# Twelve weight operands of the first four up-projection pairs, made beside the branch projections and brought by way of DRAM

## The chip, the cores and the metric

One program runs on one core of a Trainium2 chip. The metric is the device time of the program in microseconds (us), the median of several runs. Within the core five engines work side by side, each through its own instructions in order: TensorE (PE, matmuls; its weight loads are PEld), VectorE (DVE), ScalarE (ACT), GpSimd (POOL) and SyncE (SP). DMAs are issued by SP, ACT and POOL and then run by themselves. Engines wait for one another through semaphores.

## What is computed

The reference is one layer of an encoder on 1024 positions of width 1024. Its first half mixes positions by three branches, whose outputs are projected (`w_branch`), gated and added; its second half is a gated feed-forward with a conv of width 3. The two places that the change touches are these:

```python
def _token_mixer(...):
    ...
    branches = jnp.stack([o_a, o_b, o_c], axis=2)
    up = jnp.einsum('bsnw,nwd->bsnd', branches, w_branch)
    gates = jax.nn.sigmoid(gate_raw.reshape(bn, s, N_BRANCH, D_MODEL) + b_gate)
    return jnp.sum(gates * up, axis=2) @ w_o

def _conv_ffn(h, w_up, conv_w, conv_b, w_down):
    hu = _dwconv(h @ w_up, conv_w, FFN_CONV // 2) + conv_b
    a, b = jnp.split(hu, 2, axis=-1)
    return (jax.nn.silu(a) * b) @ w_down
```

`w_up` has 1024 rows and 2 x 2816 columns, which are 2 x 22 blocks of 128 columns.

## The kernel before

**Splitting.** A product of two float32 matrices is made of three matmuls. Each operand is split into a high part (a cast, on ACT) and a low part (the operand less the high part, on DVE or POOL); the matmuls are high by high, low by high and high by low. In the names `h` and `l` at the end say which part it is.

**The up-projection** goes through 22 pairs `p`: block `p` of `w_up` (of the half that goes through silu) and block 22 + `p` (the half that it is multiplied with). One pair is a 2 by 2 block matrix: two column blocks by two halves of the contraction, four raw blocks that the code calls a, b (of block `p`) and c, d (of block 22 + `p`), each 128 x 512 in memory. It is multiplied with a 2 by 2 block matrix of the activations by seven products instead of eight (`m1` to `m7`). So each pair needs operands that are sums of raw blocks: `P1` = c + d, `P3` = a + c, `P2` = P3 + d, `P4` = b + P2, besides the raw blocks A11, A12 (both in `wu1`) and A22 = d. The activations come as sums too (`T1` to `T4`, `B11`, `B21`, `B22`). A product is 12 matmuls. `m1` wants A11, `m2` A12, `m7` P3, `m6` P2, `m5` P1, `m3` A22, `m4` P4.

For each pair `up_load` (L1493) loads the two raw tiles `wur` (512 KB each) by SP and splits `wu1`; `sum_1` to `sum_4` (L1507 to L1525) make the sums in place or in `p2`; `w_split` (L1527) splits an operand, the cast on ACT and the subtraction on the engine that its caller names. For pair 2 and later `w_first` (L1536) makes P3 and P2, with sums and subtractions on DVE, and `w_later` (L1544) makes P1, A22 and P4, with sums on POOL. Pairs 0 and 1 are spread by hand over the end of the norm and the first products (L1722 to L1792), with their sums and subtractions on DVE (`pV`) and their casts on ACT (`pA`); their A22 and P4 lie in tiles named `wl`, which take buffers of the activations' tiles `F` as these come free. Each result runs through the conv (`conv`, L1795: one step on ACT and two on DVE, L1797 and L1798), and `gated` (L1807) multiplies the two halves (L1813) and stores `g_d`.

**The branch projections** of branches A and B run some 450 us before that (`ups`, L1168: 16 jobs of 24 matmuls, `up_steps`). Job by job, SP loads `wbr` (256 KB) and a gate tile (`load_gate`, L1137: 512 KB of `gt_d`, and a sigmoid on ACT, L1140); `wbr` is split into `wbh` on ACT and `wbl` on DVE; after the matmuls DVE multiplies the gate tile with the result (L1167); and after the second job of two POOL adds the two gate tiles (L1184) and stores the sum as `acc_d` (L1185). Between these matmuls run the preparations of branch C (`c_tab`, `c_prep`): transposes of `xc` into `cT`, which ACT and DVE split into `chi` and `clo` (L1104, L1105); `qpe` matmuls, whose rope is four DVE steps (L1025 to L1028) and two POOL adds (L1029, L1030); the split of the result (`n`, L1121 and L1122), its transposes `qpT`, and copies (`qp` L1096, `kpa` L1078).

**What sets the order.** TensorE's order is that of the program: where `T.kept` is set each matmul depends on the one before. Instructions that go through `pV` or `pA` keep their order among themselves in the same way. All others are placed by the framework's scheduler, which estimates when each is ready and lays out each engine's stream by that; what runs on the chip is that stream, in order. A step that waits holds up what stands behind it on its engine, the DMAs that the engine issues among them. A tile with `bufs=1` (the default where none is named) has one buffer, so its next writer waits for the last reader of the one before, for a DMA that reads it until that has landed.

## Time and profile before

| | |
|---|---|
| time, median of 3 runs | 1993.56 us (1991.68 to 1996.82) |
| the profiled execution, its own time | 1993.97 us |
| its span, first to last instruction | 1992.2 us |
| TensorE busy (matmuls) | 1928.9 us, 97% |
| TensorE's mean granted clock | 0.993 |
| DVE busy | 1280.6 us, 64% |
| ACT busy | 853.4 us, 43% |
| POOL busy | 419.7 us, 21% |
| DMA, mean | 105 GB/s |

The profile is of one execution. A row of a time line gives the start in the span, the duration, engine, line, operation, output<-inputs, and in brackets the time that the engine stood idle before and what ended that. A matmul's duration overlaps with the next one's start, so the distance of two starts is what one costs. The line of many instructions is that of a helper (L103 for those through `pV` and `pA`, L128 for matmuls, L131 for transposes, L166 and L169 for the split), so they are told apart by the tiles' names. The granted clock is a share of TensorE's full speed, 1.00 for 2.4 GHz.

### The profile page before, as it was taken

The page shows a single profiled execution, that of the slowest core. Times are in us where ns is not written, and L with a number is a line of the kernel's source. Part 1 is how long each engine was busy: PE and PEld are TensorE (multiplying, and loading weights), DVE is VectorE, ACT ScalarE, POOL GpSimd, SP SyncE. Part 2 cuts the span into 40 slices and gives each one's busy share as a digit, 9 for nine tenths or more (in the row PEclk, how much of TensorE's full clock was granted, in tenths as well). Part 3 has the DMA queues.
Part 4 walks back from the last instruction along what each step waited for, and adds up shares of the span by engine and source line. Part 5 has one row for each costly group of instructions (what it writes and reads, how often), then busy time and mean ns, then how long its engine had stood idle before and what let it go on. Part 6 is the DMA issues. An engine that isn't in the chain of part 4 may idle for free. (4 is left out here: it accounts for less than half of the span.)

```text
span 1992.2 us, 27009 instructions
## 1 busy us (share of the span) xinstructions
PE 1928.9 (97%) x10440; PEld 1606.6 (81%) x10440; DVE 1280.6 (64%) x2076; ACT 853.4 (43%) x1449; POOL 419.7 (21%) x338
## 2 busy tenths in 40 slices
PE   7998999999999999989999999998999999999998
PEld 6976887888888878868888887886888888888887
DVE  7378868666766736674467855588777677742523
ACT  6554544264254322354455543454444444532331
POOL 3321122041131111122200022103323333111110
PEclk9999999999999999999999999999999999999999
DMA  8443122122122127243500134213222222455641
GB/s 293 140 154 116 38 75 75 43 80 80 43 80 75 54 82 260 74 149 128 184 1 22 33 126 142 93 43 109 73 93 80 79 85 75 159 200 146 209 152 54
DMA packets 79203, 209.16 MB, mean 105 GB/s; under 512 B 11681, under 2 KB 17121, under 8 KB 79074
## 3 DMA queue, kind: packets, MB, share of 16 engines
q1 hardware_dynamic: 62514, 165.68, 26.2%
q10 hardware_dynamic: 14256, 33.36, 4.3%
q0 software_dynamic: 2304, 8.39, 1.1%
q8 instruction: 82, 1.34, 0.3%
q14 instruction: 47, 0.39, 0.1%
HBM read 165.62 MB, written 41.78 MB: 104 GB/s over the span
## 5 line engine op out<-in xcount | busy, mean ns | idle before, releaser
L128 PE MATMUL pj<-hhi,wth 128*128 128x512 f32 x704 | 293.8, 417 | 4.4 <-ACT u L895 1.7
L128 PE MATMUL pj<-hhi,wtl 128*128 128x512 f32 x704 | 276.8, 393 | 0.0
L128 PE MATMUL pj<-hlo,wth 128*128 128x512 f32 x704 | 275.6, 391 | 0.0
L128 PEld LDWEIGHTS pj<-hhi,wtl 128*128 128x128 f32 x704 | 132.5, 188 | 29.0
L128 PEld LDWEIGHTS pj<-hhi,wth 128*128 128x128 f32 x704 | 133.1, 189 | 25.7 <-ACT u L895 2.2
L128 PEld LDWEIGHTS pj<-hlo,wth 128*128 128x128 f32 x704 | 133.4, 189 | 20.0
L169 POOL TENSOR_TENSOR wtl<-wtr,wth 128x512 fp32r<-128x512 f32 x44 | 64.0, 1455 | 405.7 <-ACT wth L166 316.5
L169 DVE TENSOR_TENSOR gl<-gr,gh 128x512 fp32r<-128x512 f32 x38 | 29.5, 778 | 106.7 <-ACT gh L166 106.7
L128 PE MATMUL y<-wdh,gh 128*128 128x512 f32 x240 | 93.4, 389 | 0.0
L128 PE MATMUL y<-wdl,gh 128*128 128x512 f32 x240 | 93.4, 389 | 0.0
L128 PE MATMUL y<-wdh,gl 128*128 128x512 f32 x240 | 93.4, 389 | 0.0
L166 ACT CAST wth<-wtr 128x512 fp32r<-128x512 f32 x88 | 53.3, 617 | 85.8 <-PE pj L128 59.9
L128 PE MATMUL y<-wo,mg 128*128 128x512 f32 x384 | 89.2, 391 | 0.0
L605 ACT CAST tU<-pu 128x512 f16<-128x512 f32 x80 | 44.1, 587 | 102.4 <-PE pu L128 98.9
L128 PEld LDWEIGHTS y<-wo,mg 128*128 128x128 f32 x384 | 71.6, 188 | 14.7
L1520 POOL TENSOR_TENSOR wur<-wur 128x512 f32<-128x512 f32 x20 | 34.5, 1725 | 231.3 <-DVE wur L1509 192.6
L166 ACT CAST gh<-gr 128x512 fp32r<-128x512 f32 x38 | 23.7, 622 | 116.6 <-PE y L128 97.3
L610 DVE CAST tT<-pq 128x512 f16<-128x512 f32 x96 | 62.8, 684 | 16.4 <-PE pq L128 16.2
L599 DVE TENSOR_TENSOR pm<-pp,msk 128x512 f16<-128x512 f32 x96 | 63.4, 685 | 15.2 <-PE pp L128 14.5
L1388 POOL TENSOR_TENSOR g<-g,ac 128x1024 f32<-128x1024 f32 x7 | 18.4, 2629 | 217.8 <-DVE g L1167 211.2
L169 POOL TENSOR_TENSOR wdl<-wdr,wdh 128x1024 fp32r<-128x1024 f32 x12 | 29.3, 2442 | 153.7 <-ACT wdh L166 151.7
L433 ACT ACTIVATE gate<-pj,b_gate 128x512 f32<-128x512 f32 x48 | 32.9, 685 | 56.2 <-PE pj L128 56.0
(572 smaller groups left out, 5388.1 us busy)
## 6 DMA issues: line engine op xcount, KB each, us to landing
wtr<-w_t SPq DMA_DIRECT2D x44, 512.0 KB, 3.4
wur<-w_up SPq DMA_DIRECT2D x44, 512.0 KB, 3.6
wdr<-w_dn SPq DMA_DIRECT2D x44, 512.0 KB, 3.8
adaw<-w_adaT SPq DMA_DIRECT2D x64, 256.0 KB, 3.7
gt_d<-gate ACTq DMA_DIRECT2D x48, 256.0 KB, 2.0
g<-gt_d SPq DMA_DIRECT2D x24, 512.0 KB, 4.4
g_d<-cv ACTq DMA_DIRECT2D x22, 512.0 KB, 2.6
gr<-g_d SPq DMA_DIRECT2D x44, 256.0 KB, 3.3
```

The lines of the kernel that those rows point to most:

```text
L128: self.queue(self.nc.tensor.matmul(out, w, x, **kw), x, 4 if x.dtype == F32 else 1)
L166: ins = A.copy(hi, src)
L169: (eng or V).tensor_tensor(lo, src, r32(hi), op=ALU.subtract)
L433: A.activation(g, ps, AF.Identity, bias=b_gate[:, j : j + 1])
L599: V.tensor_tensor(pm, v4(pp), b4(msk[:, l, 1 - d, :]), op=ALU.mult)
L605: A.copy(nU, v4(pu))
L610: V.tensor_copy(nT, v4(pq))
L1388: G.tensor_tensor(g, g, ac, op=ALU.add)
L1520: eng.tensor_tensor(r2[:, 0:4, :], r2[:, 0:4, :], r2[:, 4:8, :], op=ALU.add)
```

## The change

A new generator `weights_ahead` runs through pairs 0 to 3. For each it loads the two raw tiles (`ua0`, `ua1`), and makes three operands: P1, A22 and P4 for pairs 0 and 1, P3, P2 and P4 for pairs 2 and 3. The sums are on DVE, the casts on ACT, the subtractions on DVE, and POOL stores each part to a DRAM tile of its own (`wx0P1h`, ..., 24 writes of 256 KB). All raw tiles and parts have one buffer each (tags `ua0`, `ua1`, `uah`, `ual`; all four have the name `ua`). `beside` takes a step of it at each odd step of `ups` after the 70th, with eight empty steps behind the loads of each pair. `w_load` later brings the parts back by SP (24 loads of 256 KB). The steps that made these operands before, on DVE, ACT and POOL, are gone; `up_load` still loads and splits as before, and pairs from 4 on are unchanged.

```diff
--- before.py
+++ after.py
@@ -1184,15 +1184,54 @@
                 G.tensor_tensor(g, held, g, op=ALU.add)
                 G.dma_start(acc_d[k], g)
 
+
+    wx_d = {}
+    sets = (("P1", "A22", "P4"),) * 2 + (("P3", "P2", "P4"),) * 2
+    for p, nms in enumerate(sets):
+        for nm in nms:
+            wx_d[p, nm] = [dram.tile([P, 4, P], F32, tag=f"wx{p}{nm}{m}", name=f"wx{p}{nm}{m}") for m in "hl"]
+
+    def weights_ahead():
+        for p, nms in enumerate(sets):
+            r1, r2 = [tp.tile([P, KT, P], F32, tag=f"ua{n}", name="ua") for n in range(2)]
+            SY.dma_start(r1, I["w_up"][p])
+            SY.dma_start(r2, I["w_up"][DFF // P + p])
+            (a, b), (c, d) = [(r[:, 0:4], r[:, 4:KT]) for r in (r1, r2)]
+            if p < 2:
+                todo = (("A22", d, None), ("P1", c, d), (None, a, c), ("P4", b, a))
+            else:
+                todo = (("P3", a, c), ("P2", a, d), ("P4", b, a))
+            for _ in range(8):
+                yield
+            for nm, o, other in todo:
+                if other is not None:
+                    V.tensor_tensor(o, o, other, op=ALU.add)
+                if nm is not None:
+                    hi, lo = (tp.tile([P, 4, P], F32R, tag=f"ua{m}", name="ua") for m in "hl")
+                    A.copy(hi, o)
+                    V.tensor_tensor(lo, o, r32(hi), op=ALU.subtract)
+                    for to, t in zip(wx_d[p, nm], (hi, lo)):
+                        G.dma_start(to, r32(t))
+                yield
+
     LATC = (36.5, 0.5, 11.7, 2.6, 1.5, 4.2, 3.0, 1.0, 2.2)
     T.kept = True
     chains.append([c_tab(), T.t + LATC[6], None])
     chains.append([c_prep(), T.t + LATC[7], None])
-    fill = ups()
+    ahead = weights_ahead()
+
+    def beside(it):
+        for n, _ in enumerate(it):
+            if n > 70 and n % 2:
+                next(ahead, None)
+            yield
+
+    fill = beside(ups())
     run(fill, "C")
     run(fill, "CK")
     for _ in fill:
         pass
+    drain(ahead)
     T.kept = False
     scE.close()
     suE.close()
@@ -1533,9 +1572,17 @@
         eng.tensor_tensor(o[1], src, r32(o[0]), op=ALU.subtract)
         yield
 
+    def w_load(p, nm, pl, bufs=4, tiles=None):
+        W[p][nm] = o = tiles or [pl.tile([P, 4, P], F32R, tag="wu" + nm, name=f"wu{nm}{m}", bufs=bufs) for m in "hl"]
+        for t, d in zip(o, wx_d[p, nm]):
+            SY.dma_start(r32(t), d)
+
     def w_first(p):
 
-        if p < NF:
+        if p < 4:
+            for nm in ("P3", "P2"):
+                w_load(p, nm, wus)
+        elif p < NF:
             sum_3(p)
             sum_2(p)
             for nm in ("P3", "P2"):
@@ -1544,10 +1591,14 @@
     def w_later(p):
         if p < NF:
             sum_1(p)
-            sum_4(p)
+            if p > 3:
+                sum_4(p)
             drain(w_split(p, "P1", wus1, eng=G))
             drain(w_split(p, "A22", wuq))
-            drain(w_split(p, "P4", wuq, bufs=2, eng=G))
+            if p > 3:
+                drain(w_split(p, "P4", wuq, bufs=2, eng=G))
+            else:
+                w_load(p, "P4", wuq, bufs=2)
 
     def prod(ps, w, x, start, cols=slice(0, 512), ks=range(4), late=None):
 
@@ -1722,7 +1773,8 @@
     m1_copy(1, pA)
     next(norm)
     wus1 = pool(hxE, "wus1", side="right")
-    w1 = [w_split(p, "P1", wus1, copy=pA.copy, eng=pV) for p in range(2)]
+    for p in range(2):
+        w_load(p, "P1", wus1)
     t2(c0)
     next(w3[1])
     next(w2[1])
@@ -1754,17 +1806,11 @@
         m6_part(p, c1, late)
         if p == 0:
             e_add(0, pV)
-            sum_1(0, pV)
-            next(w1[0])
             hi("B22", c0)
             lo("T1", c0)
             hi("B22", c1)
             lo("T1", c1)
-            next(w1[0])
-            sum_1(1, pV)
-            next(w1[1])
     e_add(1, pV)
-    next(w1[1])
     t4(c0)
     m5(0, pV)
     hi("T4", c0)
@@ -1774,22 +1820,12 @@
     m5(1, pV)
     lo("T4", c1)
 
-    late_w = []
     for p in range(2):
         w = fp.tile([P, 4, 512], F32R, tag="F", name="wl", bufs=4).rearrange("p a (k c) -> p a k c", k=4)
         for n, nm in enumerate(("A22", "P4")):
-            late_w.append(w_split(p, nm, None, copy=pA.copy, eng=pV, tiles=[w[:, n * 2], w[:, n * 2 + 1]]))
-    next(late_w[0])
-    next(late_w[0])
-    sum_4(0, pV)
-    next(late_w[1])
+            w_load(p, nm, None, tiles=[w[:, n * 2], w[:, n * 2 + 1]])
     lo("B22", c0)
     lo("B22", c1)
-    next(late_w[1])
-    sum_4(1, pV)
-    for n in (2, 3):
-        next(late_w[n])
-        next(late_w[n])
 
 
     def conv(f, ps, o):
```

TensorE's instructions stand in the same order before and after. On the other engines the order changes; the following shows four places.

POOL, at the start of the new work (`acc_d` and `g` belong to the branch projections, `rk` to branch C's rope, `wx...` are the new writes):

```order
 L1184 TENSOR_TENSOR g<-g 128x1024
 L1185 DMA acc_d<-g 128x1024
+L1214 DMA wx0A22h<-ua 128x512
+L1214 DMA wx0A22l<-ua 128x512
 L1029 TENSOR_TENSOR rk<-rk,rka 128x8x32
 L1030 TENSOR_TENSOR rk<-rk,rkb 128x8x32
+L1214 DMA wx0P1h<-ua 128x512
 L1184 TENSOR_TENSOR g<-g 128x1024
```

The writes stand between the gate adds and the rope's adds, each behind a wait for its part.

ACT, at the first `kpa` (at about 904 to 907 us before; `n_9197` and `n_9221` are the same tile):

```order
 L1096 CAST qp<-qpT 128x4x128
-L166 CAST wbh<-wbr 128x512
-L1121 CAST n_9197<-rq 128x4x64
+L1211 CAST ua<-ua 128x512
+L1121 CAST n_9221<-rq 128x4x64
+L1211 CAST ua<-ua 128x512
 L1078 CAST kpa<-kpA 128x512
 L1079 CAST kpb<-kpB 128x512
```

Two casts of new operands now stand ahead of `kpa` and `kpb`, and `wbh` stands earlier.

DVE, around the second half's `clo` (five tiles, 8756 to 8760), before:

```order
L1167 TENSOR_TENSOR g<-g,up 128x512 x2
L169 TENSOR_TENSOR wbl<-wbr,wbh 128x512
L1105 SCALAR_TENSOR_TENSOR clo_8756<-cT,cw,chi_8751 128x512
L1105 SCALAR_TENSOR_TENSOR clo_8757<-cT,cw,chi_8752 128x512
L1105 SCALAR_TENSOR_TENSOR clo_8758<-cT,cw,chi_8753 128x512
```

and after (L1208 is a sum of `weights_ahead`, L1212 a subtraction):

```order
L1212 TENSOR_TENSOR ua<-ua 128x512
L1208 TENSOR_TENSOR ua<-ua 128x512
L1212 TENSOR_TENSOR ua<-ua 128x512
L1167 TENSOR_TENSOR g<-g,up 128x512 x2
L1105 SCALAR_TENSOR_TENSOR clo_8756<-cT,cw,chi_8751 128x512
L169 TENSOR_TENSOR wbl<-wbr,wbh 128x512
L1105 SCALAR_TENSOR_TENSOR clo_8757<-cT,cw,chi_8752 128x512
L1208 TENSOR_TENSOR ua<-ua 128x512
L1212 TENSOR_TENSOR ua<-ua 128x512
L1105 SCALAR_TENSOR_TENSOR clo_8758<-cT,cw,chi_8753 128x512
```

Two operands' subtractions stand ahead of the first `clo`, and another sum and subtraction within the row.

DVE, in the second stage, from the conv of pair 1's second half to that of its first half (uB, uA), before:

```order
L1797 SCALAR_TENSOR_TENSOR cv<-uB,fcw,cv 128x1023
L1515 TENSOR_TENSOR p_13203<-wur 128x512
L1798 SCALAR_TENSOR_TENSOR cv<-uB,fcw,cv 128x1023
L1813 TENSOR_TENSOR cv<-cv 128x1024
L1533 TENSOR_TENSOR wuP3l<-wur,wuP3h 128x512
L1533 TENSOR_TENSOR wuP2l<-p_13203,wuP2h 128x512
L1797 SCALAR_TENSOR_TENSOR cv<-uA,fcw,cv 128x1023
L169 TENSOR_TENSOR wu1l<-wur,wu1h 128x1024
L1798 SCALAR_TENSOR_TENSOR cv<-uA,fcw,cv 128x1023
```

and after:

```order
L1833 SCALAR_TENSOR_TENSOR cv<-uB,fcw,cv 128x1023
L1834 SCALAR_TENSOR_TENSOR cv<-uB,fcw,cv 128x1023
L1849 TENSOR_TENSOR cv<-cv 128x1024
L1833 SCALAR_TENSOR_TENSOR cv<-uA,fcw,cv 128x1023
L1834 SCALAR_TENSOR_TENSOR cv<-uA,fcw,cv 128x1023
```

The weight steps are gone from between the conv steps; the two `wu1l` of pairs 2 and 3 now stand some 20 rows earlier, around `T2l`.

## Rows read from the trace of the kernel before

**Rows 1.** Busy time by stage: PE, PEld, DVE, ACT, POOL, clock, DMA share, GB/s.

```profile
925.00:950.00 25.00, 25.00 (x137) 21.32 (x136) 9.51 (x24) 8.80 (x14) 5.93 (x8) 1.00 0.40 136
...
1350.00:1375.00 25.00, 18.02 (x66) 13.15 (x65) 21.63 (x20) 11.44 (x18) 11.56 (x7) 0.86 0.22 82
...
1375.00:1400.00 25.00, 25.00 (x111) 20.58 (x110) 18.17 (x18) 9.93 (x13) 7.50 (x5) 1.00 0.26 88
```

**Rows 2.** TensorE's time line, second stage: start, duration, [idle before <-releaser].

```profile
1337.80 1.20 PE L128 MATMUL uB<-T4h,wl 128*128 128x512 f32 x4 [0.15 <-ACT wl L103]
...
1339.76 1.20 PE L128 MATMUL uB<-T4l,wl 128*128 128x512 f32 x4 [0.76 <-DVE T4l L103]
...
1343.23 1.19 PE L128 MATMUL uA<-B22l,wl 128*128 128x512 f32 x4 [0.43 <-DVE B22l L103]
...
1351.63 0.47 PE L128 MATMUL uA<-B11h,wu1h 128*128 128x512 f32 x1 [0.69 <-DVE cv L1798]
...
1355.12 0.50 PE L128 MATMUL uB<-T3h,wuP3h 128*128 128x512 f32 x1 [0.52 <-ACT wuP3h L1531]
...
1357.22 0.51 PE L128 MATMUL uB<-T3h,wuP3l 128*128 128x512 f32 x1 [1.36 <-DVE wuP3l L1533]
...
1364.09 0.50 PE L128 MATMUL uB<-T3h,wuP3h 128*128 128x512 f32 x1 [1.58 <-ACT wuP3h L1531]
...
1367.65 0.79 PE L128 MATMUL uB<-T3h,wuP3l 128*128 128x512 f32 x1 [2.83 <-DVE wuP3l L1533]
...
1380.40 0.39 PE L128 MATMUL uB<-T4h,wuA22h 128*128 128x512 f32 x1
```

**Rows 3.** TensorE's time line, two matmuls behind the longest wait.

```profile
1368.24 0.63 PE L128 MATMUL uB<-T3h,wuP3h 128*128 128x512 f32 x1
...
1371.66 0.63 PE L128 MATMUL uB<-T3h,wuP3l 128*128 128x512 f32 x1
```

**Rows 4.** DVE's time line, second stage: weight steps and a conv step.

```profile
1329.49 0.68 DVE L103 TENSOR_TENSOR wuP1l<-wur,wuP1h 128x512 fp32r<-128x512 f32 x1
...
1346.70 1.27 DVE L1798 SCALAR_TENSOR_TENSOR cv<-uB,fcw,cv 128x1023 f32<-128x1023 f32 x1
...
1349.08 1.21 DVE L169 TENSOR_TENSOR wu1l<-wur,wu1h 128x1024 fp32r<-128x1024 f32 x1
...
1365.85 1.75 DVE L1533 TENSOR_TENSOR wuP3l<-wur,wuP3h 128x512 fp32r<-128x512 f32 x1
```

**Rows 5.** Tile view of `wur`: ACT's casts, ns minimum, median, maximum.

```profile
L1531 ACT CAST wuP3h<-wur x20: 595/620/620, 1354.5 to 1705.6; 128x512 fp32r<-128x512 f32 x20
```

**Rows 6.** DMA issues: line, queue, count, KB each, median us to landing.

```profile
wur<-w_up SPq DMA_DIRECT2D x44, 512.0 KB, 3.6
...
gt_d<-gate ACTq DMA_DIRECT2D x48, 256.0 KB, 2.0
...
g_d<-cv ACTq DMA_DIRECT2D x22, 512.0 KB, 2.6
...
x_d<-xt POOLq DMA_DIRECT2D x8, 512.0 KB, 2.9
```

**Rows 7.** Tile view of `acc_d`: POOL's issues (ns) and landings (us).

```profile
L1185 POOL DMA_DIRECT2D acc_d<-g x8: 573/573/842, 870.5 to 977.3; - x8
...
DMA to landing us min/median/max: 3.2/4.2/6.9
```

**Rows 8.** TensorE's time line, first stage, three of its waits.

```profile
877.07 0.63 PE L131 MATMUL cT<-ident,xc 128*128 128x128 f32 x4 [0.75 <-DVE clo L1105]
...
906.91 0.66 PE L131 MATMUL qpT<-ident,n 128*128 128x128 f32 x4 [0.57 <-ACT kpa L1078]
...
957.54 0.63 PE L131 MATMUL qpT<-ident,n 128*128 128x128 f32 x4 [1.55 <-DVE n L1122]
```

**Rows 9.** DVE's and POOL's time lines at 903 us.

```profile
903.52 2.87 DVE L169 TENSOR_TENSOR wbl<-wbr,wbh 128x512 fp32r<-128x512 f32 x1
...
903.41 2.44 POOL L1184 TENSOR_TENSOR g<-g 128x1024 f32<-128x1024 f32 x1 [0.70 <-DVE g L1167]
```

## The prediction

> **What bounds the kernel now.** I read the totals first, then a table of busy time by stage, then TensorE's own time line with its waits, and the vector engine's (DVE's) rows at the same places. TensorE is busy in 97% of the span, and its instructions stand in the same order before and after the change, so only its waits and its clock can pay or cost. [rows 1] holds the stage that the change wants to relieve and the one that it loads. In the slice 1350 to 1375 TensorE is busy for 18.02 us and runs 66 instructions, where the next slice is full and runs 111; DVE is busy for 21.63 us, and the granted clock is 0.86. The waits there [rows 2] all end with DVE or with ACT feeding DVE: operands P3 of the up-projection pairs 2 and 3 (`wuP3h`, `wuP3l`) come late because the same DVE also runs the conv of pairs 0 and 1. So DVE bounds these 20 us. In the other stage, 925 to 950, TensorE is full, DVE works 9.51 us of 25, ACT 8.80 and POOL 5.93: there is room by the sum, but TensorE waits at some points for one late DVE step [rows 8].
>
> **The gain in the second stage.** The product m4 of pair 1 ends 0.69 us before the row at 1351.63, that is at 1350.94; m3 of pair 2 starts at 1380.40 [rows 2]. In between stand seven products of 12 matmuls, 84 in all. A full stage gives 111 matmuls in 25.00 us [rows 1], 0.225 us each, so the 84 need 18.9 us where 29.5 pass. The 10.6 us of excess are five waits (0.69 + 0.52 + 1.36 + 1.58 + 2.83 = 7.0), some 0.25 us at each restart (a matmul row is 0.39 long where the next starts after 0.23), and ten matmuls at half clock (0.63 long, nine of them from 1368.24 to 1371.66, one each 0.43 us [rows 3]): 10 x (0.43 - 0.225) = 2.0 us. TensorE had waited 2.83 us just before the clock fell.
>
> The change takes from DVE here the sums and the subtractions of P3 and P2 of pairs 2 and 3, eight instructions between 0.68 and 1.75 us [rows 4], and from ACT their casts of 0.62 us [rows 5]. The conv of pairs 0 and 1 stays (eight steps of 1.27 us [rows 4]), and 84 matmuls cover it. The operands now come by eight loads that SP issues at about 1324 to 1333; a load of twice the size lands in 3.6 us [rows 6], so they are there 15 us before they are used. I find no wait left between m1 and m3 of pair 2.
>
> Against it stands a small loss ahead. Two `wu1l` of pairs 2 and 3 (1.21 us each, at 1349.08 for the first [rows 4]) now stand on DVE ahead of T2's low half, and the sum of pair 2 on POOL ahead of the last row's power; that makes TensorE about 1.5 us late at 1326. But DVE no longer has the ten weight steps of 0.68 us of pairs 0 and 1 [rows 4], so the three waits of 0.15, 0.76 and 0.43 us [rows 2] shrink by as much. Followed through, m4 of pair 1 ends 0.2 us later than now. The loads of A22 and P4 of pair 0 go out once T1 is split (about 1331) and land at 1335; the first is wanted at 1337.80 [rows 2], 2.8 us of cover. Those of pair 1 land at about 1342 and are wanted at 1345.5. If a load is late here, TensorE waits one for one. Afterwards both kernels run the same pairs, bound by TensorE, so the gain stays to the end. Bounds: 7 us (a new wait of 3 us) to 10.5 us; I take 9.5, near the upper end, since the long waits are those whose cause goes away whole.
>
> **The cost in the first stage.** The twelve operands are made between 877 and 960 us. New work: 24 DVE steps of 0.68 us, 16.3 us; 12 ACT casts of 0.62 us, 7.4 us; 24 POOL issues of 0.57 us [rows 7], 13.8 us; eight loads. By the sum all of it fits into the idle time of [rows 1]. What does not fit as easily is the order. There is one high and one low tile (`uah`, `ual`), so each operand's cast and subtraction wait until the writes of the operand before have landed; and one pair of raw tiles, so each pair's load waits for the last subtraction of the pair before. These waits stand in the in-order streams of DVE, ACT, POOL and SP, among the sigmoids, the gate products, the `chi`/`clo` splits and the rope steps that TensorE needs.
>
> The length of this chain: one operand takes 0.62 + 0.68 + two issues' last (0.57 to 0.84) + landing; a new pair's raw load adds 3.6 [rows 6] + 0.68 = 4.3 us, four times 17.2. The landing of a 256 KB write from POOL is in no row. ACT's writes show that half the size saves 0.6 us (2.6 for 512 KB, 2.0 for 256 KB [rows 6]); so from POOL's 512 KB rows it is 2.9 - 0.6 = 2.3 us (`x_d`, a quiet stage [rows 6]) to 4.2 - 0.6 = 3.6 us (`acc_d`, this very stage, median), with 6.9 - 0.6 = 6.3 us as its slowest [rows 7]. I take 3.6, since `acc_d` leaves the same engine at the same time. An operand then costs 0.62 + 0.68 + 0.7 + 3.6 = 5.6 us, and the chain 12 x 5.6 + 17.2 = 84 us; with 2.3 us it is 69, with 4.4 us 94. The room is 877.07 to 957.54 [rows 8], 80.5 us. So at my value the chain is as long as its room, and a step in it comes late at some places. The ones I find by putting the new rows between the old times: ACT's cast of A22 of pair 1 stands ahead of `kpa` at 906 to 908 (about 1.7 us for TensorE, which waited 0.57 us there already [rows 8]), casts and subtractions of P1 and P4 of pair 1 ahead of the first `clo` at about 922 (2 to 3 us), raw loads of pairs 2 and 3 ahead of the gate loads on SP, and the last operands ahead of the last rope and gate products (before 957.54). Delays at one place are partly absorbed by the next, since TensorE falls back with them. Sum: 1 us when landings take 2.3 to 2.8 us, 3 to 8 at 3.6 to 4.4; I take 4.5. Whatever TensorE loses here is carried to the end.
>
> DVE's steps are longer beside POOL's work: `wbl` took 2.87 us while POOL added two gate tiles [rows 9], where a subtraction of that size takes 0.68 [rows 4]. The Trainium skill ("SBUF — State Buffer", Who interferes with whom) says that a DVE instruction with two SBUF inputs contends with a GpSimd instruction that reads SBUF; the row agrees, and the new subtractions have two such inputs. If three of the 24 meet an add, that is 3 x 1.1 (0.68 to 1.75, [rows 4]) = 3 us of DVE time, within its idle half; it is in the 4.5.
>
> The two transfers' own weight (6.3 MB written and read) I cost at nothing, as the DMA engines are busy for 0.40 of the time in 925 to 950 [rows 1]; without that cover it shows as longer landings, which are bounded above.
>
> **The sum.** The profiled run took 1993.97 us (span 1992.2), 0.4 above the median of 1993.56. 1993.97 - 9.5 + 4.5 = 1988.97, on the median **1988.5**, 0.25% less. A measurement here can tell 0.3%, 6 us, from no change.
>
> **Rivals.** (1) The first stage hides all of it. If writes land in 2.8 us or less the chain is under 75 us in 80.5. For it: the sums of idle time, and `x_d`'s 2.9; against it: `acc_d`. Time 1993.6 - 9.5 = 1984. The Trainium skill ("DMA: Bandwidth & Descriptors", Anatomy of one DMA — SWDGE (gpsimd) path) fits a DMA from this queue by 2.0 us plus bytes over 436 GB/s; as an estimate that is 2.6 us for 256 KB, and the sum by it is this rival's. `x_d` agrees with it (3.2 by the fit), `acc_d` is 1 us above.
>
> (2) The write chain overruns, and the kernel is slower. The mechanism: the same one-buffer chain, with landings stretched by the gate loads and by DVE. TensorE takes half to all of the overrun. To lose 9.5 + 6 us the chain must be 96 us (all) to 111 us (half), that is landings of 4.6 to 5.9 us: above `acc_d`'s median, under its slowest of 6.9. At 5.5 us the chain is 107 us, 26 over, TensorE 13 to 26: about 2003. Long waits also cost clock, as at 1368. For it: 24 waits in four in-order streams, each of which holds up everything behind it; against it: TensorE is the bound there and the others run ahead of it.
>
> (3) The second stage gives back only half: a load (P1, or A22 and P4) is late on SP, or T4 and B22 are late since DVE's order changed. 1993.6 - 5 + 4.5 = 1993. For it: SP has 24 more issues in one in-order queue, some held by landings; against it: the covers of 2.8 us and more.
>
> **How the numbers follow.** Forecast (net -2 to -8) 0.45; rival 1 0.22; rival 2 0.16; rival 3 0.17. The forecast's own range is 1985.5 to 1991.5, and about 0.18 of its chance lies below 1987.6; with rival 1 that makes faster 0.40. Rival 2 above 1999.5 gives slower 0.15; the rest, 0.45, is within 0.3%. Range 1983 (rival 1 with 10.5 us) to 2000, which leaves out the worse part of rival 2.
>
> **What would show it.** The second stage is right if 1350 to 1375 has TensorE full at clock 1.00 and no wait for `wuP3l`. The first stage is right if DVE and ACT wait for landings of `wx...` writes, of 3 to 4 us, and TensorE's new waits between 900 and 962 (on `kpa`, `clo`, `n`, `wbl`) add to 3 to 8 us. It is wrong if these waits are under 1 us, if they exceed 10, or if TensorE waits for `wl`, `wuP1h` or `wuP3h` from a DMA after 1330.

## The result, and the profile after

| | before | after |
|---|---|---|
| median, same session | 1995.19 us (1991.68 to 1996.85) | 2007.81 us (2005.17 to 2012.37) |
| profiled execution, its time | 1993.97 us | 2008.40 us |
| its span, its clock | 1992.2 us | 2006.6 us, 0.991 |

The change makes the kernel slower: ratio 1.0066, 95% interval 1.0051 to 1.0080. That is 12.6 us on the median, where 5 us of gain was forecast, and 8 us above the upper end of the range.

TensorE's instructions stand in the same order in both kernels, so the start of each matmul can be compared with its own start before. The shift (after minus before, in us; the time is that of before):

| time | 700 | 860 | 1000 | 1300 | 1340 | 1380 to the end |
|---|---|---|---|---|---|---|
| shift | 0.1 | 6.7 | 21.7 | 20.3 | 25.8 | 14.6 |

Three pieces matter. Between 860 and 1000, where the operands are made, 15.0 us are lost. Ahead of pair 0, between 1300 and 1340, another 5.5 go. Between 1340 and 1380 the kernel gains 11.2. The 6.7 us up to 860 are not a step of the change: until SP issues the first new load, at 867.8, all five engines run the same instructions in the same order in both traces. There the sixteen variants below scatter between -1 and +8, and undisturbed single executions of the kernel before lie between 1990 and 2000 us. I use shifts for where time goes inside one stage, and ratios for verdicts.

Busy time by stage, after (PE, PEld, DVE, ACT, POOL, clock, DMA share, GB/s):

```profile
925.00:950.00 25.00, 20.48 (x105) 16.84 (x104) 13.64 (x19) 8.51 (x14) 6.10 (x8) 0.93 0.69 210
950.00:975.00 25.00, 21.70 (x104) 16.23 (x102) 18.51 (x31) 7.89 (x14) 11.84 (x17) 1.00 0.56 190
...
1350.00:1375.00 25.00, 23.51 (x116) 19.86 (x116) 18.20 (x17) 9.41 (x11) 2.84 (x2) 0.97 0.50 165
1375.00:1400.00 25.00, 25.00 (x112) 20.52 (x111) 16.14 (x17) 11.86 (x16) 4.56 (x3) 1.00 0.32 106
```

Against [rows 1], the early stage is no longer full (20.48 of 25 us, 105 matmuls for 137), although DVE, ACT and POOL are each idle for 11 us or more of that slice. The late one is full at clock 1.00 in 1375 to 1400, which now holds what stood at 1350 to 1385 before.

TensorE's larger waits after (start, duration, idle before and what ended it), four of the early stage and two of the late one:

```profile
915.36 0.66 PE L131 MATMUL qpT<-ident,n 128*128 128x128 f32 x4 [2.43 <-ACT kpa L1078]
...
934.37 0.70 PE L131 MATMUL cT<-ident,xc 128*128 128x128 f32 x4 [4.52 <-DVE clo L1105]
...
961.79 0.73 PE L128 MATMUL up<-oah,wbh 128*128 128x512 f32 x2 [1.42 <-ACT wbh L166]
...
977.51 0.63 PE L131 MATMUL qpT<-ident,n 128*128 128x128 f32 x4 [3.02 <-DVE n L1122]
...
1347.23 0.66 PE L128 MATMUL uA<-T2h,wuP2h 128*128 128x128 f32 x4 [1.80 <-ACT T2h L103]
...
1365.41 1.20 PE L128 MATMUL uB<-T4l,wl 128*128 128x512 f32 x4 [1.49 <-DVE T4l L103]
```

All waits of TensorE from 870 to 1000 add to 19.9 us; before they added to 8.8. That is 11.1 more. The rest of the 15 I put down to the restarts behind these waits and to a clock of 0.93 in 925 to 950. In the late stage the five waits of [rows 2] on `wuP3` and the conv are gone. What made the wait on `clo` can be read off DVE's time line:

```profile
921.03 0.69 DVE L1212 TENSOR_TENSOR ua<-ua 128x512 fp32r<-128x512 f32 x1 [3.03 <-DMA wx0P4l<-ua]
...
931.77 0.69 DVE L1212 TENSOR_TENSOR ua<-ua 128x512 fp32r<-128x512 f32 x1 [5.68 <-DMA wx1P1l<-ua]
932.38 1.28 DVE L1167 TENSOR_TENSOR g<-g,up 128x512 f32<-128x512 f32 x2
933.57 0.75 DVE L1105 SCALAR_TENSOR_TENSOR clo<-cT,cw,chi 128x512 fp32r<-128x512 f32 x1
```

DVE stood 5.68 us for a write's landing. Queued behind were a gate product and `clo`, for which TensorE stood 4.52 us. The wait on `wbl` at 983.18 stands behind such a landing too:

```profile
980.63 0.69 DVE L1212 TENSOR_TENSOR ua<-ua 128x512 fp32r<-128x512 f32 x1 [3.27 <-DMA wx3P2l<-ua]
...
983.18 0.73 PE L128 MATMUL up<-oah,wbl 128*128 128x512 f32 x2 [1.37 <-DVE wbl L169]
```

The other waits do not go back to a landing in this way. Ahead of `kpa` ACT stood for DVE, whose subtraction itself stood behind gate products and splits:

```profile
914.20 0.62 ACT L1211 CAST ua<-ua 128x512 fp32r<-128x512 f32 x1 [3.31 <-DVE ua L1212]
914.72 0.58 ACT L1078 CAST kpa<-kpA 128x512 fp32r<-128x512 f32 x1
```

The waits on `wbh` (1.42) and on the `n` at 970.07 (1.02) stand behind POOL's gate add, which stood behind the write of `wx2P4h`, for which POOL waited 1.78 us for ACT's cast. The wait on the `n` at 977.51 (3.02) has a new subtraction right ahead of the rope steps that `n` needs, stretched beside POOL's gate add. DVE, then POOL:

```profile
972.23 2.89 DVE L1212 TENSOR_TENSOR ua<-ua 128x512 fp32r<-128x512 f32 x1
...
971.80 2.77 POOL L1184 TENSOR_TENSOR g<-g 128x1024 f32<-128x1024 f32 x1 [0.98 <-DVE g L1167]
```

So of TensorE's waits 5.9 us (4.52 + 1.37) stand right behind a landing. The other new ones stand behind casts, writes and sums of the same chain that came at a bad place.

The transfers (count, KB each, median us to landing; of the 24 writes three are shown):

```profile
ua<-w_up SPq DMA_DIRECT2D x8, 512.0 KB, 5.5
...
wx0P1h<-ua POOLq DMA_DIRECT2D x1, 256.0 KB, 2.3
...
wx0P4l<-ua POOLq DMA_DIRECT2D x1, 256.0 KB, 6.5
...
wx1P1l<-ua POOLq DMA_DIRECT2D x1, 256.0 KB, 5.9
```

Over the 24 writes the landing is 2.3 to 6.5 us, 4.35 in the median; the raw loads take 5.5, where the quiet stage of [rows 6] had 3.6. With these the prediction's own chain is 12 x (0.62 + 0.68 + 0.7 + 4.35) + 4 x (5.5 + 0.68) = 101 us; the trace has 98.6, from the first cast at 883.0 to the last write's issue at 981.6.

### The profile page after: what moved, and what is told of

The parts are those of the page before. It is cut to its first block, busy times and chain, and to the rows that moved or that the text cites. A ratio compares the mean times of both kernels' runs of the same rounds, so it can differ in the third digit from the quotient of the medians.

```text
span 2006.6 us, 27138 instructions
## 1 busy us (share of the span) xinstructions
PE 1934.0 (96%) x10440; PEld 1609.1 (80%) x10440; DVE 1292.0 (64%) x2082; ACT 855.2 (43%) x1449; POOL 425.3 (21%) x358
## 5 line engine op out<-in xcount | busy, mean ns | idle before, releaser
L128 PEld LDWEIGHTS pj<-hlo,wth 128*128 128x128 f32 x704 | 134.2, 191 | 20.3
L610 DVE CAST tT<-pq 128x512 f16<-128x512 f32 x96 | 62.8, 685 | 16.0 <-PE pq L128 15.8
```

Of the source, the lines that this page charges most:

```text
L128: self.queue(self.nc.tensor.matmul(out, w, x, **kw), x, 4 if x.dtype == F32 else 1)
L610: V.tensor_copy(nT, v4(pq))
```

## Which half costs, which half pays

**first_only** makes and writes the twelve operands, and loads none. It is the changed kernel with the second stage as it was:

```diff
-        if p < 4:
-            for nm in ("P3", "P2"):
-                w_load(p, nm, wus)
-        elif p < NF:
+        if p < NF:
...
-    for p in range(2):
-        w_load(p, "P1", wus1)
+    w1 = [w_split(p, "P1", wus1, copy=pA.copy, eng=pV) for p in range(2)]
```

> The twelve operands are made and written as in the change, but nothing is brought back: pairs 0 to 3 make their operands as before. Theory (write chain): the chain of single buffers is as long as in the changed kernel (about 99 us from the first cast to the last write, room 80), and TensorE takes the overrun: 15 us between 850 and 1000, nothing after 1300, so about 2010 against 1995. Rival (crowding: the new instructions and transfers as such slow the stage): the same 15 us, so this run measures the cost by itself and does not part the two. A second rival says that the 6.6 us which TensorE had already lost at 850 in the profile of the changed kernel belong to the change: then 22 us, about 2017, and 6 us at 850 again; if they are scatter of single executions, the shift at 850 is another here.

Measured: 2009.93 against 1994.23, ratio 1.0073 (1.0055 to 1.0091). The shift goes from 5.1 at 860 to 20.9 at 1000 and stays there. The rival that counts the shift at 860 to the change had expected about 2017.

**second_only** makes one operand, and every load reads its two tiles:

```diff
+    sets = (("A22",),)
...
-        for t, d in zip(o, wx_d[p, nm]):
+        for t, d in zip(o, wx_d[0, "A22"]):
```

> One operand is made and written (A22 of pair 0); all 24 later loads read its two tiles in DRAM, so the up-projection of pairs 0 to 3 is computed with wrong weights, with all its instructions. This is the second stage by itself. Theory: TensorE gains 10.5 us between 1350 and 1400 and loses 4 to 5 us ahead of it, where POOL's sum and the two wu1l stand in front of the last row's steps: net -5 to -6, and under 1 us lost at 850 to 1000: about 1990 against 1995. Rival (the loads collide with the raw loads): the gain is under 8 us with waits on DMA for wl or wuP1h, about 1993.

Measured: 1992.55, ratio 0.9986 (0.9974 to 0.9999). The shift is 5.8 at 1300, 13.0 at 1340, 1.7 at 1380: 7.1 lost, 11.2 gained. So the first stage alone holds the slowdown (+15.7 on the median of first_only), and the second pays less than it could because of a loss ahead of it.

## What the first stage's 15 us are

**act_writes**: ACT issues the 24 writes.

```diff
-                        G.dma_start(to, r32(t))
+                        A.dma_start(to, r32(t))
```

> The change, with the 24 writes issued by ACT in place of POOL. Theory (write chain): ACT's writes of 256 KB landed in 2.0 us where POOL's took 4.4 at the median, so an operand takes about 4.0 us in place of 6.4 and the chain about 73 us in place of 99, within its room of 80: the loss of 15 us falls to 5 or less, total about 1993 to 1996. Rival (crowding): the same number of instructions, transfers and bytes, with 24 issues now in ACT's own stream: the loss stays at 12 us or more, total 2003 or more.

Measured: 2006.43, ratio 1.0053 (1.0035 to 1.0071); first stage +18.8. A miss. From ACT's queue the landings are 2.0 to 8.0 us, 3.6 in the median of the 22 that the trace has, so most of the landing wasn't POOL's queue; and ACT now stands for DVE ahead of its issues. ACT's time line (ACTq is its issue), then TensorE's:

```profile
910.76 0.33 ACTq L1214 DMA_DIRECT2D wx0P4l<-ua  x1
911.18 0.62 ACT L1211 CAST ua<-ua 128x512 fp32r<-128x512 f32 x1 [4.28 <-DVE ua L1212]
911.71 0.58 ACT L1078 CAST kpa<-kpA 128x512 fp32r<-128x512 f32 x1
...
912.34 1.11 PE L131 MATMUL qpT<-ident,n 128*128 128x128 f32 x4 [8.26 <-ACT kpa L1078]
```

The wait on `kpa` grew from 2.43 to 8.26 us.

**first_other_src** and **first_no_write** were meant to separate waiting from moving. Both are first_only; the one writes blocks that lie ready, so that the high and low tiles wait for no landing, and the other writes nothing:

```diff
-                    for to, t in zip(wx_d[p, nm], (hi, lo)):
-                        G.dma_start(to, r32(t))
+                    for to, t in zip(wx_d[p, nm], (oah, oal)):
+                        G.dma_start(to, r32(t[0])[:, 0:512].rearrange("p (a c) -> p a c", a=4))
```

> The first stage by itself, as in first_only (which cost 15.7 us), but the 24 writes take their 256 KB from tiles that nobody overwrites in this stage (oah, oal), so no cast or subtraction waits for a landing, while instructions, transfers and bytes are the same. Nothing reads what is written. Theory (the waits for landings in in-order streams make the loss): the loss falls from 15.7 to 5 us or less, about 1999. Rival (the transfers slow the gate and weight loads of the stage): it stays at 12 us or more, 2006 or more.

> The first stage by itself without its 24 writes: raw loads, sums, casts and subtractions stay, and nothing uses their results. Both theories of first_other_src expect a loss of 4 us or less here, about 1998. A third (the 36 new steps of DVE and ACT and the raw loads make the loss by themselves, by their place in the streams) expects 8 us or more, 2002 or more.

Measured: 1998.16 against 1994.92, ratio 1.0008 (0.9997 to 1.0018), shift in the stage -0.9; and 1996.95, ratio 1.0015 (1.0002 to 1.0029), +2.0. Busy time of 925 to 950 in first_only, then in first_other_src:

```profile
925.00:950.00 25.00, 21.13 (x112) 17.05 (x111) 15.41 (x25) 7.93 (x13) 7.33 (x11) 1.00 0.72 226
```

```profile
925.00:950.00 25.00, 25.00 (x138) 21.25 (x136) 21.45 (x37) 11.63 (x19) 8.77 (x8) 1.00 0.65 208
```

TensorE is full again. But first_other_src did not do what it was made for. As its sources lay ready, POOL issued all 24 writes ahead of the stage, the last one 44 us before ACT's first new cast:

```profile
820.25 0.78 POOL L1213 DMA_DIRECT2D wx0A22h<-oah  x1 [0.37 <-ACT oah L166]
...
838.48 0.54 POOL L1213 DMA_DIRECT2D wx3P4l<-oal  x1
...
883.09 0.62 ACT L1210 CAST ua<-ua 128x512 fp32r<-128x512 f32 x1 [1.72 <-DMA ua<-w_up]
```

So both runs are the stage without writes in it. What they show is this. The 36 steps of DVE and ACT and the eight raw loads cost -0.9 and 2.0 us by the shifts, 1.6 and 3.0 by the ratios. The 24 writes, with all that waits for them, make the rest: 12 to 13 of first_only's 14.6 us by the ratios. And not all of the waits come from the writes: TensorE waits 2.4 and 2.1 us for `kpa` here too.

How the cost of the writes parts into waits for landings, POOL's or ACT's stands at the issues, and the traffic, these runs don't show. The trace of after has the first two, as read above. Against the traffic as the price speak four_src and four_act below: without and with eight writes in the stage they lose the same. For 24 writes that is not shown. Two sets of high and low tiles would take away most waits for landings; that wasn't tried.

## What the loss ahead of the second stage is

In the trace of after, POOL's time line and then DVE's, ahead of pair 0:

```profile
1332.36 1.31 POOL L1559 TENSOR_TENSOR wur<-wur 128x512 f32<-128x512 f32 x1 [0.64 <-DMA wur<-w_up]
1333.64 1.01 POOL L1494 TENSOR_TENSOR s<-s,mhalf 128x1 f32<-128x1 f32 x1
1343.67 2.31 POOL L1559 TENSOR_TENSOR wur<-wur 128x512 f32<-128x512 f32 x1 [9.03 <-DMA wur<-w_up]
```

```profile
1334.68 0.75 DVE L103 TENSOR_SCALAR x<-xt,s 128x1024 f32<-128x1024 f32 x1 [0.46 <-POOL s L1494]
...
1344.77 1.76 DVE L103 SCALAR_TENSOR_TENSOR F<-F,F 128x512 f32<-128x512 f32 x1
...
1347.21 0.69 DVE L103 TENSOR_TENSOR T2l<-F,T2h 128x512 fp32r<-128x512 f32 x1 [0.69 <-ACT T2h L103]
```

The sum for pair 2 stands ahead of the power `s` that the last row's `x` needs; the sum for pair 3 runs beside the product `F` on the way to T2, which takes 1.76 us where it took 0.69 before. The Trainium skill ("SBUF — State Buffer", Who interferes with whom) names this meeting of a two-input DVE instruction and a reading GpSimd, and the rows agree.

**sum_fix** is second_only with the first sum of pairs 2 and 3 put on DVE, behind the activations; **second_fix** moves the `wu1l` subtractions there too:

```diff
-            sum_1(p)
+            sum_1(p, pV if p < 4 else G)
...
-        split(o[0], o[1], r[0])
+        split(o[0], o[1], r[0], pV if p in (2, 3) else None)
```

> As second_only (wrong weights in pairs 0 to 3), with the sums of P1 of pairs 2 and 3 on DVE behind the activations, in place of POOL, and the two wu1l of 1.21 us still early. If POOL's sums beside DVE make most of the 7 us ahead of 1350: 2 us or less are lost there, about 1987. If the two wu1l make it: 4 us or more are lost, about 1991.

> As second_only (one operand made, all loads read it, wrong weights in pairs 0 to 3), with the subtractions of wu1 and the sums of P1 of pairs 2 and 3 kept on DVE behind the steps of the activations that the program has ahead of them, in place of DVE's and POOL's early places. Theory (these early steps, and the sums on POOL beside DVE, make the loss ahead of 1350): the 7 us that second_only lost between 1310 and 1345 fall to 2 or less and the gain of 11 us behind it stays at 8 or more, about 1986. Rival (T2 and T4 are late for another reason, as the loads in SP's queue): 4 us or more are still lost, about 1991.

Measured: sum_fix 1987.36, ratio 0.9960 (0.9948 to 0.9973), loss ahead 1.2 us; second_fix 1986.56, ratio 0.9954 (0.9938 to 0.9971), no loss ahead, gain 11.8. So the two sums on POOL made most of the 5 to 7 us, and the early `wu1l` the rest.

**after_fix** is the whole change with these two edits:

> The whole change, with the subtractions of wu1 and the sums of P1 of pairs 2 and 3 kept on DVE behind the activations' steps, as in second_fix. Theory: the two stages add up. The first still costs 15 us, the second gives 10 in place of 5.7, so 4 to 6 us less than the changed kernel's 2007.8: about 2003. Rival (TensorE's lateness in the first stage hides what second_fix gained): within 2 us of 2007.8.

Measured: 1998.76 against 1994.98, ratio 1.0018 (1.0008 to 1.0028). It is 9 us better than the change, where 4 to 6 were expected. Its first stage still loses 15.8, and its second gives 11.8; the sum of the two, 4.0, fits the ratio, which is 3.6 us.

## Fewer operands, other places

**pairs23** makes the six operands of pairs 2 and 3 alone, since the waits of [rows 2] were theirs:

```diff
-    sets = (("P1", "A22", "P4"),) * 2 + (("P3", "P2", "P4"),) * 2
+    sets = {2: ("P3", "P2", "P4"), 3: ("P3", "P2", "P4")}
```

> Only the six operands of pairs 2 and 3 (P3, P2, P4) are made ahead and brought by way of DRAM, by POOL as in the change; pairs 0 and 1 are as before. Theory (write chain): six operands and two raw loads make a chain of about 50 us, which fits the room: loss at 850 to 1000 of 3 us or less, gain at 1350 to 1400 of 8 to 10 us: about 1988 to 1991. Rival (crowding, in proportion to the operands): a loss of 7 to 8 us: about 1993 to 1996.

Measured: 1992.63 against 1994.23, ratio 0.9983 (0.9972 to 0.9995); first stage +4.9, second -9.6. The loss lies between the two theories. Most of the gain (9.6 of 11.2) needs only these six.

**spaced23** gives each of its steps more room, one behind each twelfth piece of the up projection, pinned behind that matmul:

```diff
-            if n > 70 and n % 2:
+            if n > 70 and n % 12 == 0:
...
-                    A.copy(hi, o)
+                    behind(A.copy(hi, o))
```

> As pairs23 (six operands, pairs 2 and 3), but its steps come at each twelfth step of the branch projections, and are kept by the scheduler behind the matmuls at which the program makes them, so that an operand follows the one before by 7 us or more and no write is still under way. Theory (waits for landings): the 4.9 us that pairs23 lost between 850 and 1000 fall to 2 or less, the gain of 9.6 us at 1350 to 1400 stays, about 1986 to 1988. Rival (crowding, traffic): the loss stays at about 5 us, about 1990.

Measured: 2001.49, ratio 1.0033 (1.0020 to 1.0046), first stage +12.9. A miss. No step waits for a write's landing any more, but other stands have come: SP's issue of pair 3's raw load waits for the last subtraction of pair 2, with gate loads queued behind it, and POOL's writes wait for ACT's casts. One row each of the waits by cause, SP from 890 to 960 and POOL from 890 to 975 (total, times, longest):

```profile
SPq L1200 <- DVE ua L1214: 5.2, 1, 5.2
...
POOL wx2P4h L1216 <- ACT ua L1213: 10.7, 1, 10.7
```

**four** therefore takes the wait on SP away as well: a ring of four raw blocks, only P3 and P2 of pairs 2 and 3, one step behind each eighteenth piece.

```diff
+            t = tp.tile([P, 4, P], F32, tag="ua", name="ua", bufs=4)
+            behind(SY.dma_start(t, I["w_up"][f][:, k * 4 : k * 4 + 4]))
...
+            if n > 70 and n % 18 == 0:
```

> Only the four operands P3 and P2 of pairs 2 and 3 go by way of DRAM; their raw blocks come singly into a ring of four buffers of 256 KB, so that the next block's load waits for a sum long past, and the steps come at each 18th step of the branch projections, kept behind TensorE's matmuls there. P1 and P4 of pairs 2 and 3 are summed on POOL (P4 with one sum more). Theory (only waits for landings cost): a loss of 2 us or less at 850 to 1000, and 8 to 10 us gained at 1350 to 1400, about 1987 to 1989, faster than both kernels. Rival (anything placed into that stage costs): 5 us lost as in pairs23, about 1990 to 1991.

Measured: 1996.19 against 1994.98, ratio 1.0006 (0.9996 to 1.0017); +7.9 in the first stage, -8.3 in the second (P4 stays on POOL). A miss again. POOL's time line:

```profile
928.12 0.56 POOL L1185 DMA_DIRECT2D acc_d<-g  x1 [0.30 <-POOL g L1184]
940.68 0.55 POOL L1210 DMA_DIRECT2D wx2P2h<-ua  x1 [12.00 <-ACT ua L1207]
```

POOL had reached its write early and stood 12 us for ACT's cast, with the rope sums, the gate add and `acc_d` behind it. Two variants take that stand away: **four_src** writes blocks that lie ready, **four_act** lets ACT issue.

```diff
-                G.dma_start(to, r32(t))
+                behind(A.dma_start(to, r32(t)))
```

> As in the run 'four' (P3 and P2 of pairs 2 and 3, a ring of four raw blocks, a step behind each eighteenth piece of up-projection work), but the eight writes take tiles that lie ready (blocks of other operands), so GpSimd has no cast to wait for and nothing waits for a landing; pairs 2 and 3 get wrong weights in P3 and P2 (the time read is that of the same traffic and the same arithmetic). Theory A, that what 'four' lost at 850 to 1000 us (7.9 us) was GpSimd's stand of 12.00 us for the cast of its own write, with the g add and the accumulator write behind it: TensorE loses 0 to 2 us there, the later gain of 8.3 stays, time 1986 to 1990 us. Theory B, that anything placed into that stage costs what 'four' cost, by VectorE's and ScalarE's added work and the traffic: a loss of 6 or more there, time 1994 to 1997 us.

> As 'four', with the right weights, but ScalarE issues each pair of writes itself behind its cast, in place of GpSimd; ScalarE then waits for VectorE's subtraction before it issues the second write. Theory A (GpSimd's stand was the loss): the stand of 12 us on GpSimd is gone, ScalarE stands for the subtraction a microsecond or two per operand instead; TensorE loses 2 to 4 us at 850 to 1000 us, time 1988 to 1992 us, at or below the kernel before. Theory B (any work placed there): 6 us or more lost, time 1994 to 1997 us.

Measured, against 1995.46: 1993.71, ratio 0.9993 (0.9983 to 1.0004), and 1994.41, ratio 0.9992 (0.9982 to 1.0002); 4.9 and 4.8 us lost. Neither theory had it right: the stand was some 3 of the 7.9, and 5 remain. In four_src the eight writes again left POOL ahead of the stage (817.5 to 821.5), so its equal loss speaks against a price of eight writes in the stage as such. In both traces the same row of events ends in a wait of TensorE for `n`, of 3.17 and 3.67 us, at the matmul that waited 1.55 before [rows 8]. From four_act, DVE, POOL, ACT and TensorE:

```profile
953.57 2.89 DVE L1205 TENSOR_TENSOR ua<-ua 128x512 f32<-128x512 f32 x1
...
953.18 2.73 POOL L1184 TENSOR_TENSOR g<-g 128x1024 f32<-128x1024 f32 x1 [5.49 <-ACT qp L1096]
...
958.71 0.40 ACT L1121 CAST n<-rq 128x256 fp32r<-128x256 f32 x1 [1.59 <-POOL rq L1030]
...
959.72 1.08 PE L131 MATMUL qpT<-ident,n 128*128 128x128 f32 x4 [3.67 <-DVE n L1122]
```

DVE's sum takes 2.89 us beside POOL's add; the rope products, POOL's `rq` sums, `n` and TensorE stand behind it one after the other, and the clock is 0.86 in 950 to 975.

Three more test that reading: the steps at two other places of the round (**four_act6**, **four_act12**), and the four sums on POOL (**four_actp**), where they can't meet POOL's own add.

```diff
-            if n > 70 and n % 18 == 0:
+            if n > 70 and n % 18 == 6:
```

```diff
-            behind(V.tensor_tensor(o, o, other, op=ALU.add))
+            behind(G.tensor_tensor(o, o, other, op=ALU.add))
```

> As 'four_act', but each step stands behind the sixth piece of up-projection work in a round of eighteen, so elsewhere in the order of VectorE, ScalarE and SyncE. Theory A (in 'four_act' the loss is one meeting: VectorE's sum of a raw block, 0.6 us alone, took 2.89 us beside GpSimd's g add, and the rotary products, GpSimd's rq sums, ScalarE's cast n and TensorE's wait of 3.67 us stand behind it in a row): the loss at 850 to 1000 us changes with the place; 0 to 2 us if no sum of over 1 us stands ahead of the rotary products, with about 3 us for each that does; time 1986 to 1990 us in the first case. Theory B (the added work costs 5 us wherever it stands): 4 to 6 us again, 1993 to 1996 us.

> As 'four_act6', behind the twelfth piece of eighteen. Theory A: the loss at 850 to 1000 us follows the number of sums of over 1 us that stand ahead of rotary products (about 3 us each, 0 to 2 us without one). Theory B: 4 to 6 us as at the other places, 1993 to 1996 us.

> As 'four_act', but the four sums of raw blocks are GpSimd's in place of VectorE's (on GpSimd such a sum of 128x512 takes 1.3 to 2.3 us in the second stage). Theory A: VectorE no longer stands 2.89 us for the sum, but GpSimd's own sums stand ahead of its rq sums, and it waits for the raw block's landing in its order; a loss of 1 to 4 us at 850 to 1000 us, time 1988 to 1993 us. Theory B: 4 to 6 us as before, 1993 to 1996 us.

Measured, against 1994.60: four_act6 1992.57, ratio 0.9992 (0.9982 to 1.0003); four_act12 1995.42, 0.9999 (0.9988 to 1.0009); four_actp **1988.59**, 0.9969 (0.9958 to 0.9981). In four_actp the first stage costs nothing any more (shift 6.4 at 860, 6.1 at 1000) and the second still gains 8.3, counted to the end. Its DVE and POOL lines at the place of the meeting, then its busy time:

```profile
957.68 2.87 DVE L1208 TENSOR_TENSOR ua<-ua 128x512 fp32r<-128x512 f32 x1
...
954.38 1.30 POOL L1205 TENSOR_TENSOR ua<-ua 128x512 f32<-128x512 f32 x1
...
957.28 2.71 POOL L1184 TENSOR_TENSOR g<-g 128x1024 f32<-128x1024 f32 x1 [1.61 <-ACT ua L1207]
```

```profile
950.00:975.00 25.00, 24.16 (x115) 19.27 (x113) 14.65 (x27) 11.59 (x20) 9.26 (x9) 1.00 0.70 221
```

A subtraction still meets the add and takes 2.87 us, but the sum of 1.30 us no longer stands on DVE as well, TensorE waits 0.23 us for `n` where it waited 3.67, and the clock stays at 1.00. This version is 6 us faster than the kernel before, about the gain that the prediction wanted from the whole change. The other two don't fit one price per meeting: four_act6 has a sum of 2.09 us and loses 0.5 to 2 us in its trace, yet its median gained only 2.0 us; four_act12 has one sum of 2.88 us, priced at 3, and loses 10. There POOL also stood 11.15 us for ACT, which stood for gate loads and for DVE. So the place changes the loss in single traces, from 0.5 to 10 us, but the ratios of four_act, four_act6 and four_act12 can't be told apart (0.9992, 0.9992, 0.9999). What moving the sums to POOL gains is shown by the ratios; that the meeting ahead of `n` is the reason is read off the traces.

## Why the prediction was wrong, by its own steps

**The gain in the second stage was right.** 10.6 us of excess were counted from the waits, the restarts and the half clock, and 9.5 taken; 11.2 came back here and in second_only, and 11.8 net of the loss ahead in second_fix. No load came late, and the waits on `wuP3` are gone.

**The small loss ahead was mis-sized.** 1.5 us, shrinking to 0.2, was the term; 5.5 were lost, and under 1 us of it was absorbed before 1350. The prediction named POOL's sum ahead of the power, but not that the other sum would slow DVE's `F` beside it, nor that both sit on the way to operands for which TensorE already waits. The second stage as a whole gave 14.6 - 20.3 = -5.7, not -9.5.

**The cost in the first stage is the step that failed.** The term was 4.5, bounded by 8; 15.0 was measured (15.8 in first_only). The mechanism was the one that the prediction names, waits of a one-buffer chain in in-order streams; four parts of its size went wrong.

First, a row was misread. [rows 7] is the view of the tile `acc_d`: its landings mix POOL's eight writes with the eight loads by which SP brings `acc_d` back later. The view of the issues of the kernel before has the two apart:

```profile
acc_d<-g POOLq DMA_DIRECT2D x8, 512.0 KB, 5.0
...
ac<-acc_d SPq DMA_DIRECT2D x8, 512.0 KB, 3.9
```

A 512 KB write of this stage landed in 5.0 us, not in 4.2. Less 0.6 that is 4.4 for 256 KB, and 4.35 was measured. With the row read rightly the prediction's own chain is its 94 us, for which it would have charged 8, its upper bound.

Second, raw loads were taken from a quiet stage at 3.6 and were 5.5. That makes 101 us, against a room of 80.5. In the stage without writes they took 3.9 and 3.7 (first_other_src, first_no_write), where first_only has 5.0, so the writes lengthened them. Third, the reading of the overrun: "partly absorbed by the next" was the choice, and TensorE paid 15 us where the overrun was 18 (98.6 less 80.5), 0.8 of it if all is set against the chain. Fourth, the meetings with POOL: three of the 24 new DVE steps met an add, as supposed, but they took 3.31, 1.57 and 2.89 us, 5.7 more than alone and not 3, and the last of them stood right ahead of the rope steps.

Rival 2 had this mechanism, with half to all of the overrun; the prediction gave it 0.16, held down by the misread `acc_d`. Its point of decision, landings of 4.6, was reached with 4.35 because raw loads had grown with them.

The Trainium skill ("DMA: Bandwidth & Descriptors", Anatomy of one DMA — SWDGE (gpsimd) path) would have put a landing at an estimated 2.6 us. That is the median of the twelve writes in pairs23, and 1.75 less than that of the 24 here; the eight POOL writes of four took 3.6. For the 512 KB of `acc_d` the prediction has 3.2 by the fit and calls `acc_d` 1 us above it; by the right row it is 1.8 above.

**The idle sums misled.** "By the sum all of it fits" was true of the steps: first_no_write does them for 2 to 3 us. What counted was who stands in front of whom, and for what.

**The sum.** 1993.97 + 6.7 (ahead of any new step) + 15.0 - 1.4 (given back by 1300, where before had a slice at clock 0.93) + 5.5 - 11.2 = 2008.6, and the profiled run took 2008.40. That the terms add up says nothing of the 6.7, which are what is left. No step of the change lies ahead of them, and no experiment was made on them. Over the seventeen changed versions the ratio less the stages leaves 2 us in the median; for the change itself it leaves 5, so about that much of the distance to the forecast has no cause shown.

## What to carry to other kernels

In this case work put into idle time cost little by its length and much by what it waited for: give each added step inputs that are ready and buffers that are free when the engine reaches it, or the stand is passed on to everything queued behind it. When a chain of one buffer is about as long as its room, price it with landings of a loaded stage, and don't count on the overrun being absorbed; here TensorE paid 0.8 of it. A tile's view mixes all transfers that touch the tile, so take a landing from a view that names the issue. And look where a variant's new instructions ended up before reading its time: first_other_src and four_src had their writes elsewhere. Move the fewest operands that remove the wait: four of the twelve gave 8 of the 11 us, and with their sums on the other engine the stage that holds them lost nothing.

## What the runs showed of the hardware

- Which engine issues a 256 KB write changed its landing less than expected in this loaded stage: 2.3 to 6.5 us from POOL with a median of 4.35, 2.0 to 8.0 from ACT with 3.6. The number of writes alone doesn't order the landings: from POOL the median was 4.35 with 24 of them, 2.6 with 12 (pairs23) and 3.6 with 8 (four).
- A subtraction or sum of 128x512 on DVE takes 0.68 us alone. Beside an add of POOL it ends 0.54 to 0.56 us after that add ends, in each meeting shown here: at 903.52 in [rows 9], and at 972.23, 1344.77 (a product), 953.57 and 957.68. So it costs what is left of POOL's instruction, here up to 2.6 us. In after it was so even where DVE had begun 0.34 us before POOL:

```profile
953.87 3.31 DVE L1212 TENSOR_TENSOR ua<-ua 128x512 fp32r<-128x512 f32 x1
...
954.21 2.40 POOL L1184 TENSOR_TENSOR g<-g 128x1024 f32<-128x1024 f32 x1
```

- On POOL the same sum takes 1.30 us, so the slower engine was the better place.
